# Two-layer decoder trunk on one core: all of GpSimd's transfers move to SyncE's queue, the convolution's columns are requested first, and the pool of big tiles has 24 places, not 22

## The chip, the core and the metric

The kernel runs on one core of a Trainium2 chip. The core has a matrix engine (TensorE, PE in the profile; its weight loads are PEld), a vector engine (VectorE, DVE), a scalar engine (ScalarE, ACT), GpSimd (POOL) and SyncE (SP), which here only issues transfers. Each engine takes its instructions in the order of the program; a name with a q (SPq, ACTq) is the engine's queue, where transfers are issued and waits are kept. All transfers run on the same 16 DMA engines. The metric is the time of one execution on the device in microseconds (us); compared are medians of several runs.

## What is computed

Two layers over 256 tokens of width 1024. Layer 0 mixes tokens with a convolution module, layer 1 with causal attention; beside it each has attention into 256 memory tokens. Each is followed by a projection, a norm, a mixture of experts (4 groups of 8, the best group and in it the best two experts per token) and a second norm.

```python
for i in range(DEPTH):                       # DEPTH = 2
    if i % 2 == 0:
        u = x @ conv_w_in                    # gated, then 31 taps along the tokens, norm, silu
        y_mix = conformer_conv(u[..., :2 * MIX_WIDTH], conv_dw_w, conv_dw_b, conv_ln_g, conv_ln_b)
    else:
        u = x @ moba_w_in
        y_mix = moba_attention(q, k, v)      # causal; one block of 256 tokens
    y_mem = memory_attention(q_mem, mem_k, mem_v)
    y = concatenate([y_mix, y_mem]) @ w_o[i]
    x = layer_norm(ALPHA * x + y, ln1_g[i], ln1_b[i])
    f = hierarchical_moe(x, w_rg[i], b_rg[i], w_re[i], b_re[i], w_gate[i], w_up[i], w_down[i])
    x = layer_norm(ALPHA * x + f, ln2_g[i], ln2_b[i])
```

All 64 experts are computed on slots of tokens, so every weight is read: 3 x 2 MB for an expert, 447 MB in all.

## The kernel before

**The pool and the loads.** Weights come in loads of 1 MB, each into a tile of 128 x 2048 numbers from one pool, `big`, of NB = 22 tiles (L41, L91). Activations take tiles from the same pool (`act`, L150). The order of loads is a list (`want`, L249 to L274): six tiles of the convolution's input weights, the memory tokens, four tiles around them, four of w_o (14 loads up to here), the gains, then the experts of layer 0, and so on for layer 1. A load is issued at the earliest point of the program at which a tile is sure to be free at every later point: the program is walked once without issuing anything, which leaves for each point the number of loads that may be out, NB less the tiles that activations hold plus the tiles that are done with (L147, L80), lowered to the least of all later points; `pump` (L137) then issues up to that number. By this count 14 loads may be out from the start until the third gated block of the convolution, and 37 of the first layer's when the norm ahead of its experts is done. Loads 16 to 39 are those of four experts whose number is fixed (kind "s"); load 40 is the first whose expert is chosen at run time, so that it waits for the numbers `eid`, which VectorE writes at L1208, and is let into the list by `opened` (L1209).

**Queues.** The weights, the input `raw`, the tokens `xn` and the router's weights are issued by SP. ScalarE issues one transfer: the convolution's columns (L552: taps, bias, gains, 204 KB), after the first two casts of the input and ahead of the first cast of a weight (`split`, L344), which TensorE's first matmuls (L405) need. GpSimd issues the rest: in the convolution stage the gated activations `h` of each of three blocks go to a buffer `hd` in DRAM (L597, two transfers a block) and come back shifted as `hs` (L617, eight a block), for the matmuls at L626 (`conv`). The program calls conv(0) and conv(1) in the middle of block 2, conv(2) and conv(3) after the memory keys, conv(4) and conv(5) between the two attentions into memory. GpSimd also writes the memory keys and values to DRAM (L722), from where layer 1 loads them.

**The tokens.** `xn` is loaded at L685, behind the router's weights (`router_load`, L324), and first used by `residual` (L498, with matmuls at L496).

**The branch.** In the middle of each layer's experts (after group 4) stands a branch (L1395) on the count of experts with more tokens than slots. Its body (`overflow`, L1251) holds up to seven more experts, whose weights GpSimd loads in 512-wide pieces (L1290).

Of the kernel before, what the change touches and what calls it, by code (L numbers as in the profile page):

```python
# [9 lines left out]
BF = mybir.dt.bfloat16  # L10
# [3 lines left out]
OP = mybir.AluOpType  # L14
# [3 lines left out]
S = 256  # L18
D = 1024
NT = S // 128  # L20
# [3 lines left out]
P = 128  # L24
MIX = 768
MC = MIX // 128
# [11 lines left out]
NEG = -1e30  # L38
FAR = 1e5
HW = 288  # L40
NB = 22  # L41
LATE = 1
NQ = 7
REST = (5, 6, 8, 10)
# [41 lines left out]
def body(ctx, tc, ahead, xT0, xs, memT, w_mem_kv, conv_w_in, conv_cols, moba_w_in, w_o, gains, w_r,  # L86
# [159 lines left out]
    raw = act("raw")  # L246
    for h in range(2):
        nc.sync.dma_start(raw[:, h * 1024:(h + 1) * 1024], xT0[:, h * 1024:(h + 1) * 1024])
    for b in range(3):  # L249
        for i in range(2):  # L250
            want(("cv", b, i), load(conv_w_in, 2 * b + i))
# [36 lines left out]
    nc.vector.tensor_scalar(alpha, ident, ALPHA, None, op0=OP.mult)  # L288
    upper = t1("upper")
    nc.vector.tensor_scalar(upper[:, :P], diff[:, :P], 0.0, None, op0=OP.is_gt)  # L290
    cmask = keep.tile([P, P], BF, name="cmask")
    nc.vector.tensor_scalar(cmask, upper[:, :P], NEG, None, op0=OP.mult)
    ident_b = keep.tile([P, P], BF, name="ident_b")
    nc.vector.tensor_copy(ident_b, ident)
    upper_b = keep.tile([P, P], BF, name="upper_b")
    nc.vector.tensor_copy(upper_b, upper[:, :P])
    ones_b = keep.tile([P, P], BF, name="ones_b")
# [120 lines left out]
    def attend(items, causal, room=None):  # L418


        n0 = 128 if causal else 256
        spans = [(0, n0), (n0, n0 + 256)]
        heads = []
        for qT, kT, v, put in items:
            two = [pb(), pb()]
            for s_ in two:
                if causal:
                    for a, b in spans:
                        nc.tensor.matmul(s_[:, b - P:b], lhsT=ident_b, rhs=cmask, start=a == 0, stop=False)
            for t in range(NT):  # L430
                a, b = spans[t]
                cuts = [(a, b - P), (b - P, b)] if causal else [(a, b)]
                for c, d in cuts:
                    for hh, s_ in enumerate(two):
                        r = slice(hh * HD, (hh + 1) * HD)
                        if d > c:
                            nc.tensor.matmul(s_[:, c:d], lhsT=qT[r, t * P:(t + 1) * P], rhs=kT[r, c - a:d - a],
                                             start=not causal and t == 0, stop=t == NT - 1 and d == b)
            heads += two
        done_ = []  # L440
        pr_ = room() if room else act("apr").rearrange("p (h s) -> p h s", h=4)
        for s_ in heads:
            st = small([P, 8], "ast", bufs=4)
            pr = pr_[:, len(done_)]
            for t in range(NT):
                a, b = spans[t]
                nc.vector.tensor_reduce(st[:, t:t + 1], s_[:, a:b], axis=AX.X, op=OP.max)
            nc.vector.tensor_scalar(st[:, 2:4], st[:, 0:2], -1.0, None, op0=OP.mult)
            for t in range(NT):
                a, b = spans[t]  # L450
                nc.scalar.activation(pr[:, a:b], s_[:, a:b], AF.Exp, bias=st[:, 2 + t:3 + t],
                                     scale=1.0, accum_out=st[:, 4 + t:5 + t])
            done_.append((st, pr))
        for st, pr in done_:
            nc.vector.reciprocal(st[:, 6:8], st[:, 4:6])
            for t in range(NT):
                a, b = spans[t]
                nc.vector.tensor_scalar(pr[:, a:b], pr[:, a:b], st[:, 6 + t:7 + t], None, op0=OP.mult)
        blocks = [(kt, t) for kt in range(2) for t in range(NT) if not causal or kt <= t]
        for i in range(len(items)):  # L460
            yield
            for hh in range(2):
                pr = done_[2 * i + hh][1]
                p_ = pb()
                for n, (kt, t) in enumerate(blocks):
                    a = spans[t][0] + kt * P
                    nc.tensor.transpose(p_[:, n * P:(n + 1) * P], pr[:, a:a + P], ident)
                n = len(blocks)
                evac(pr[:, :n * P], p_[:, :n * P])
        yield  # L470
        for i, (qT, kT, v, put) in enumerate(items):
            y_ = pb()
            for t in range(NT):
                kts = [kt for kt, t_ in blocks if t_ == t]
                for kt in kts:
                    n = blocks.index((kt, t))
                    for hh in range(2):
                        r = slice(hh * HD, (hh + 1) * HD)
                        nc.tensor.matmul(y_[r, t * P:(t + 1) * P], lhsT=v[:, kt, r],
                                         rhs=done_[2 * i + hh][1][:, n * P:(n + 1) * P], start=kt == kts[0],  # L480
                                         stop=kt == kts[-1])
            put(y_[:, :256])
        if not room:
            free()
# [56 lines left out]
    def conv_layer():  # L541
        acc = Acc()
        xT = parted(raw, "xT", (nc.scalar.copy, nc.vector.tensor_copy))
        free()
        cv_ = act("cv")
        cv = cv_[:, :MC * S].rearrange("p (c s) -> p c s", c=MC)
        npc, nwr = MC * (CW + 5), MC * 32
        cols = cv_[:, MC * S:MC * S + npc + nwr]
        pct = cols[:, :npc].rearrange("p (c k) -> p c k", c=MC)
        wrc = cols[:, npc:].rearrange("p (c b q) -> p c b q", c=MC, b=4)  # L550
        id32 = cv_[:, 2048 - 32:]
        nc.scalar.dma_start(cols, conv_cols)  # L552
        hd = dr.tile([MC, P * HW], F32, name="hd")
        wdg, hsrc, hs = {}, {}, {}

# [18 lines left out]
        def glu(b):  # L574
# [19 lines left out]
                nc.vector.tensor_mul(h[:, CW - 1:CW - 1 + S], p_[:, k], sg[:, k])  # L594
                hsrc[2 * b + i] = h
            for i in range(2):
                nc.gpsimd.dma_start(hd[2 * b + i].rearrange("(p s) -> p s", p=P), hsrc[2 * b + i])  # L597
            shifted(b)

        def last_taps(b):  # L600
# [11 lines left out]
        def shifted(n):  # L612

            for c in (2 * n, 2 * n + 1):
                hs[c] = act("hs")[:, :4 * HW].rearrange("p (b s) -> p b s", b=4)
                for r in range(4):
                    nc.gpsimd.dma_start(hs[c][32 * r:32 * r + 32, :, :HW - 4],  # L617
                                        view(hd[c, r:], [[HW, 32], [32 * HW, 4], [1, HW - 4]]))

        def conv(c):  # L620
# [17 lines left out]
        mT = parted(held("mem"), "mT")  # L638
        done("mem")
        taps(1)  # L640
        glu(2)

        p_ = pb()
# [36 lines left out]
        next(ats[0])  # L680
        conv(4)
        router_load(0)
        for t in range(NT):
            for half in range(2):
                nc.sync.dma_start(xn[t][half], xs[t, half])  # L685
        feed.ahead(2)
        next(ats[1])
        conv(5)
# [30 lines left out]
                                           op1=OP.mult, accum_out=col[:, t:t + 1])  # L719
        rsqrt(col[:, 2:4], col[:, 0:2])  # L720
        for i, v in enumerate((memk, memv)):
            nc.gpsimd.dma_start(kvd[:, i * 512:(i + 1) * 512].rearrange("p (c s) -> p c s", c=2), v)  # L722
        for a in ats:
            next(a)
        for a in ats:
# [317 lines left out]
    def moe(l, mixer, after=None):  # L1043
# [207 lines left out]
        def overflow():  # L1251
# [26 lines left out]
            def one_more(q):  # L1278
# [2 lines left out]
                sq = so[:, 4:8] if q else so[:, 0:4]  # L1281
                gather(one_hot(sq), xg=xo)
                pt = spots_turned(spots(sq))
                r = nc.gpsimd.value_load(ids[0:1, q:q + 1], min_val=l * NE, max_val=l * NE + NE - 1)

                def piece(src):
                    count[0] += 1
                    i = count[0] % 3
                    t_ = t2("wpc") if i == 2 else room[:, J * P + i * 512:J * P + (i + 1) * 512]
                    nc.gpsimd.dma_start(t_, src)  # L1290
                    return t_

                def up_piece(a):
# [183 lines left out]
```

## Time and profile before

| | |
|---|---|
| median of 3 runs | 1175.22 us (1174.49 to 1183.54) |
| the profiled execution | 1182.57 us, of which its span 1180.9 us |
| granted TensorE clock, mean | 0.947 |
| busy: PE, PEld, DVE, ACT, POOL | 1028.2, 722.3, 366.4, 210.5, 60.6 us |
| bytes moved | 447.16 MB, mean 379 GB/s over the span |

The page shows the span in 40 slices of 29.5 us. Busy PE is no proof of a bound by PE, since a matmul that waits for its weights inside the pipeline counts as busy; which limit holds in a stage is read from the bytes per slice and from the waits. The convolution stage lasts to about 160 us, the first experts to about 590, the attention stage to about 735, the second experts to the end.

### The profile page before, as it was taken

Reading aid. Unit: us, or ns where it says so; the run is one execution under the profiler, and the core shown is the slowest. Engines: PE = TensorE matmul, PEld = TensorE weight load, DVE = VectorE, ACT = ScalarE, POOL = GpSimd, SP = SyncE. Lnnn points to the kernel's source line nnn. Section 1 sums busy time; section 2 is a strip of 40 time slices with the busy share of each in tenths; the row PEclk is TensorE's granted clock in tenths of the full one; section 3 lists DMA queues with packets and bytes.
Section 4 is the critical chain, followed back from the end, with each engine's and each line's share of the span. In section 5 each row is a group of like instructions: output and inputs, shape, how many; then the busy total and the mean of one; then the engine's idle time right before and its main releaser. Section 6 shows DMA issues by size and latency. Waiting matters only on the chain. (4 is left out here: it accounts for less than half of the span.)

```text
span 1180.9 us, 26574 instructions
## 1 busy us (share of the span) xinstructions
PE 1028.2 (87%) x11292; PEld 722.3 (61%) x11292; DVE 366.4 (31%) x936; ACT 210.5 (18%) x456; POOL 60.6 (5%) x152
## 2 busy tenths in 40 slices
PE   1998999999889998866589998999997999996775
PEld 1986766665565575544469986666545656654542
DVE  3576832221121121111065765222211211221103
ACT  2314411111010010001044532011010111110000
POOL 1440200000000000000020002000000000000001
PEclk9999989999999999889899997999998999997777
DMA  9686969999999999999997386999999999999994
GB/s 381 235 282 265 347 251 419 424 424 426 425 424 425 427 424 425 426 426 425 425 427 271 108 293 252 384 425 424 426 427 422 425 427 425 424 426 425 426 425 177
DMA packets 63656, 447.16 MB, mean 379 GB/s; under 512 B 7656, under 2 KB 8040, under 8 KB 10280
## 3 DMA queue, kind: packets, MB, share of 16 engines
q1 hardware_dynamic: 61640, 439.73, 90.2%
q0 software_dynamic: 1600, 4.90, 1.5%
q8 instruction: 92, 1.51, 0.5%
q10 hardware_dynamic: 288, 0.73, 0.2%
q14 instruction: 36, 0.29, 0.1%
HBM read 442.87 MB, written 2.46 MB: 377 GB/s over the span
## 5 line engine op out<-in xcount | busy, mean ns | idle before, releaser
L974 PE MATMUL pb<-w,xg 128*32 128x128 f32 (+2 forms) x6528 | 400.1, 323 | 87.3 <-DMA w<-in_w_gate_dram 51.0
L974 PEld LDWEIGHTS pb<-w,xg 128*32 128x32 f32 (+2 forms) x6528 | 276.6, 123 | 208.9 <-issue 82.8
L1026 PE MATMUL pb<-w,hT 128*32 128x256 f32 (+1 forms) x1600 | 157.5, 432 | 7.8 <-DMA w<-in_w_down_dram 3.1
L1026 PEld LDWEIGHTS pb<-w,hT 128*32 128x32 f32 (+1 forms) x1600 | 74.5, 116 | 62.9 <-issue 36.5
L1031 ACT COPY o<-pb 32x256 f32<-32x256 f32 (+2 forms) x104 | 43.2, 416 | 367.1 <-DVE o L1031 232.5
L405 PE MATMUL pb<-xT,hl 128*128 128x256 f32 x672 | 86.0, 290 | 25.8 <-ACT hl L344 25.6
L1031 DVE COPY o<-pb 32x256 f32<-32x256 f32 (+2 forms) x104 | 49.8, 478 | 177.6 <-PE pb L1026 157.7
L998 DVE TENSOR_TENSOR h<-pb,h 128x128 f32<-128x128 f32 (+2 forms) x64 | 22.9, 358 | 253.8 <-PE pb L974 246.8
L405 PEld LDWEIGHTS pb<-xT,hl 128*128 128x128 f32 x672 | 84.0, 198 | 27.3 <-ACT hl L344 25.6
L496 PE MATMUL pa<-o,pt 128*128 128x512 f32 x192 | 92.7, 628 | 3.5 <-DVE o L1031 2.0
L950 PEld LDWEIGHTS pb<-oh,xn 128*128 128x128 f32 x704 | 80.6, 192 | 7.4 <-issue 7.4
L950 PE MATMUL pb<-oh,xn 128*128 128x128 f32 x704 | 84.0, 278 | 0.0
L345 DVE TENSOR_TENSOR hl<-w,hl 128x1024 fp32r<-128x1024 f32 x53 | 63.1, 1221 | 36.0 <-ACT hl L344 33.1
L496 PEld LDWEIGHTS pa<-o,pt 128*128 128x128 f32 x192 | 37.7, 207 | 44.5 <-issue 32.4
L344 ACT CAST hl<-w 128x1024 fp32r<-128x1024 f32 x54 | 54.7, 1053 | 33.3 <-DMA w<-in_memT_dram 19.3
L992 ACT ACTIVATE h<-pb 128x128 f32<-128x128 f32 (+2 forms) x64 | 21.2, 331 | 195.9 <-PE pb L974 195.0
L128 POOL TENSOR_SCALAR lmv<-lmv 128x1 f32<-128x1 f32 x8 | 1.7, 216 | 1027.7 <-DVE lmv L506 1026.0
L496 PE MATMUL pa<-hl,y 128*128 128x512 f32 x192 | 46.0, 395 | 0.0
L125 DVE COPY hT<-pb 128x128 f32<-128x128 f32 (+2 forms) x32 | 11.4, 358 | 105.1 <-PE pb L1004 81.2
L123 ACT COPY xg<-pb 128x512 f32<-128x512 f32 x22 | 12.9, 586 | 160.4 <-PE pb L950 160.4
L496 PEld LDWEIGHTS pa<-hl,y 128*128 128x128 f32 x192 | 35.5, 188 | 8.0 <-issue 0.5
L1238 DVE TENSOR_SCALAR ow<-iota,sm,sw 128x128 f32<-128x128 f32 x96 | 26.8, 343 | 19.2 <-PEq L1395 13.3
(229 smaller groups left out, 705.9 us busy)
## 6 DMA issues: line engine op xcount, KB each, us to landing
w<-in_w_gate_dram SPq DMA_DIRECT2D x128, 1024.0 KB, 19.5
w<-in_w_up_dram SPq DMA_DIRECT2D x128, 1024.0 KB, 19.5
w<-in_w_down_dram SPq DMA_DIRECT2D x128, 1024.0 KB, 19.5
w<-in_moba_w_in_dram SPq DMA_DIRECT2D x10, 1024.0 KB, 18.4
w<-in_w_o_dram SPq DMA_DIRECT2D x8, 1024.0 KB, 19.8
w<-in_conv_w_in_dram SPq DMA_DIRECT2D x7, 1024.0 KB, 15.4
w<-in_gains_dram SPq DMA_DIRECT2D x4, 1024.0 KB, 12.4
hs<-hd POOLq DMA_DIRECT2D x24, 142.0 KB, 3.2
```

What stands on the lines that cost most here:

```text
L123: nc.scalar.copy(o, i)
L344: nc.scalar.copy(hi, src)
L345: eng.tensor_sub(lo, src, hi.bitcast(F32))
L405: nc.tensor.matmul(o, lhsT=lhs(a, j), rhs=rhs(b, j), start=k == 0, stop=k == 3 * n - 1)
L496: nc.tensor.matmul(self.at[t][half], lhsT=lhsT, rhs=rhs, start=start, stop=stop)
L950: nc.tensor.matmul(p_[:, j - jj], lhsT=now(t, j), rhs=oh[t], start=t == 0, stop=t == NT - 1)
L974: nc.tensor.matmul(o_[b * n:(b + 1) * n, :], lhsT=self.xs[:, j, :], rhs=wj[:, pairs(b) if fw == P else slice(b * fw, (b + 1) * fw)], start ...
L992: nc.scalar.activation(self.h[:, :fw], g_, AF.Silu)
L998: nc.vector.tensor_mul(self.h[:, :fw], u_, self.h[:, :fw])
L1026: nc.tensor.matmul(ds[0][b * n:(b + 1) * n, :dw], lhsT=chunk(c), rhs=wd(c, b * dw, (b + 1) * dw), start=c == 0, stop=c == 3)
L1031: (nc.scalar.copy if 2 * b >= m else nc.vector.tensor_copy)(o[lo:lo + n, b * D // m:(b + 1) * D // m], ds[b] if nb == 1 else ds[0][b * n:( ...
L1238: nc.vector.tensor_scalar(o_[:, t], iota, sm[:, i:i + 1], sw[:, 4 + i:5 + i], op0=OP.is_equal, op1=OP.mult)
```

## The change

The columns' tile is taken and its transfer issued ahead of the list of loads, still by ScalarE. The transfers of `h`, `hs` and the memory keys and values, and the pieces and the expert's number in the overflow's body, are issued by SP. The tokens are requested in the program after the taps of block 1, ahead of the third gated block, and no longer behind the router's weights. NB is 24. The scratch space that transfers issued by GpSimd need in every partition is set to 256 bytes, which makes room for the two tiles. The causal mask is added as a product of -1e30 times the identity and a 0/1 triangle, not of the identity and a triangle of -1e30; one tile of constants is gone.

```diff
-NB = 22
+NB = 24
...
     raw = act("raw")
     for h in range(2):
         nc.sync.dma_start(raw[:, h * 1024:(h + 1) * 1024], xT0[:, h * 1024:(h + 1) * 1024])
+    cv_ = act("cv")
+    ncol = MC * (CW + 5), MC * 32
+    nc.scalar.dma_start(cv_[:, MC * S:MC * S + sum(ncol)], conv_cols)
     for b in range(3):
...
-    cmask = keep.tile([P, P], BF, name="cmask")
-    nc.vector.tensor_scalar(cmask, upper[:, :P], NEG, None, op0=OP.mult)
-    ident_b = keep.tile([P, P], BF, name="ident_b")
-    nc.vector.tensor_copy(ident_b, ident)
+    neg_b = keep.tile([P, P], BF, name="neg_b")
+    nc.vector.tensor_scalar(neg_b, ident, NEG, None, op0=OP.mult)
...
-                        nc.tensor.matmul(s_[:, b - P:b], lhsT=ident_b, rhs=cmask, start=a == 0, stop=False)
+                        nc.tensor.matmul(s_[:, b - P:b], lhsT=neg_b, rhs=upper_b, start=a == 0, stop=False)
...
-        cv_ = act("cv")
...
-        nc.scalar.dma_start(cols, conv_cols)
...
-                nc.gpsimd.dma_start(hd[2 * b + i].rearrange("(p s) -> p s", p=P), hsrc[2 * b + i])
+                nc.sync.dma_start(hd[2 * b + i].rearrange("(p s) -> p s", p=P), hsrc[2 * b + i])
...
-                    nc.gpsimd.dma_start(hs[c][32 * r:32 * r + 32, :, :HW - 4],
+                    nc.sync.dma_start(hs[c][32 * r:32 * r + 32, :, :HW - 4],
...
         taps(1)
+        for t in range(NT):
+            for half in range(2):
+                nc.sync.dma_start(xn[t][half], xs[t, half])
         glu(2)
...
         router_load(0)
-        for t in range(NT):
-            for half in range(2):
-                nc.sync.dma_start(xn[t][half], xs[t, half])
...
-            nc.gpsimd.dma_start(kvd[:, i * 512:(i + 1) * 512].rearrange("p (c s) -> p c s", c=2), v)
+            nc.sync.dma_start(kvd[:, i * 512:(i + 1) * 512].rearrange("p (c s) -> p c s", c=2), v)
...
-                r = nc.gpsimd.value_load(ids[0:1, q:q + 1], min_val=l * NE, max_val=l * NE + NE - 1)
+                r = nc.sync.value_load(ids[0:1, q:q + 1], min_val=l * NE, max_val=l * NE + NE - 1)
...
-                    nc.gpsimd.dma_start(t_, src)
+                    nc.sync.dma_start(t_, src)
...
-    nc = _bacc.Bacc("TRN2", target_bir_lowering=False, num_devices=1)
+    nc = _bacc.Bacc("TRN2", target_bir_lowering=False, num_devices=1, dynamic_dma_scratch_size=256)
```

## Rows read from the trace of the kernel before

**Rows 1.** The page, GB/s moved in each of 40 slices of the span

```profile
GB/s 381 235 282 265 347 251 419 424 424 426 425 424 425 427 424 425 426 426 425 425 427 271 108 293 252 384 425 424 426 427 422 425 427 425 424 426 425 426 425 177
```

**Rows 2.** The chain that ended last, two pieces: start us, us, what

```profile
979.18 19.04 DMA w<-in_w_down_dram
...
1143.53 19.41 DMA w<-in_w_down_dram
```

**Rows 3.** Timeline of SP, its first waiting issues: start us, us, line, out<-in, count

```profile
9.40 0.33 SPq L183 DMA_DIRECT2D w<-in_conv_w_in_dram  x1
...
14.26 7.74 SPq L183 DMA_DIRECT2D w<-in_w_o_dram  x4
```

**Rows 4.** Queues (packets, MB, share); issues (KB, median us to landing); hs min/median/max

```profile
q0 software_dynamic: 1600, 4.90, 1.5%
...
w<-in_w_gate_dram SPq DMA_DIRECT2D x128, 1024.0 KB, 19.5
...
hd<-h POOLq DMA_DIRECT2D x6, 144.0 KB, 2.1
...
DMA to landing us min/median/max: 2.7/3.2/8.0
```

**Rows 5.** Timeline of the start, ACT and PE, with idle time and its releaser

```profile
24.09 0.38 ACTq L552 DMA_DIRECT2D cv<-in_conv_cols_dram  x1
24.50 5.78 ACT L344 CAST hl<-w 128x1024 fp32r<-128x1024 f32 x6 [19.27 <-DMA w<-in_memT_dram]
...
25.60 31.77 PE L405 MATMUL pb<-xT,hl 128*128 128x256 f32 x240 [25.60 <-ACT hl L344]
```

**Rows 6.** Timeline of the convolution's blocks, POOL, PE and SP

```profile
41.80 1.33 POOL L597 DMA_DIRECT2D hd<-h  x2 [37.95 <-DVE h L594]
...
44.72 4.49 POOL L617 DMA_DIRECT2D hs<-hd  x8 [1.57 <-ACT hl L344]
...
57.30 6.25 PE L626 MATMUL pb<-hs,wdg 128*32 128x256 f32 x112
...
60.59 0.33 SPq L189 DMA_DIRECT2D w<-in_gains_dram  x1
...
75.18 6.25 PE L626 MATMUL pb<-hs,wdg 128*32 128x256 f32 x112
```

**Rows 7.** The wait for xn, and busy us, clock, DMA share, GB/s behind it

```profile
99.82 5.40 PE L496 MATMUL pa<-xn,alpha 128*128 128x512 f32 x8 [3.25 <-DMA xn<-in_xs_dram]
...
100.00:102.00 2.00, 2.00 (x3) 0.78 (x4) 2.00 (x3) 0.77 (x1) 0.00 (x0) 0.52 1.03 367
```

**Rows 8.** Timeline at the first layer's gate: SP's issues, and the expert numbers

```profile
138.94 9.21 SPq L213 DMA_DIRECT2D w<-in_w_up_dram  x2
...
160.00 3.02 SPq L213 DMA_DIRECT2D w<-in_w_down_dram  x2
...
160.81 0.18 DVE L1208 TENSOR_SCALAR eid<-pb 1x32 int32<-1x32 f32 x1 [4.86 <-PE pb L1201]
...
166.52 2.07 SPq L213 DMA_DIRECT2D w<-in_w_gate_dram  x2
```

**Rows 9.** Busy us by engine, clock, DMA share and GB/s ahead of that gate

```profile
156.00:160.00 4.00, 4.00 (x28) 2.90 (x27) 0.00 (x0) 1.17 (x2) 0.00 (x0) 0.74 0.00 0
```

**Rows 10.** Timeline of SP at the second layer's gate

```profile
710.88 10.20 SPq L213 DMA_DIRECT2D w<-in_w_up_dram  x2
733.10 3.02 SPq L213 DMA_DIRECT2D w<-in_w_down_dram  x2
```

**Rows 11.** The branch at L1395: duration ns min/median/max, first and last start; SP's issues

```profile
L1395 POOLq INC_SWDGE_SEM  x2: 801/812/822, 166.2 to 739.2; - x2
L1395 SPq COMPARE_BRANCH  x2: 45/49/53, 309.3 to 882.1; - x2
...
L1395 PEldq COMPARE_BRANCH  x2: 6038/6090/6142, 311.2 to 884.7; - x2
...
308.92 8.95 SPq L213 DMA_DIRECT2D w<-in_w_up_dram  x2
```

More of the change, by code (lines that the diff above doesn't have):

```diff
@@ L544, in conv_layer @@
         free()
-        cv_ = act("cv")
         cv = cv_[:, :MC * S].rearrange("p (c s) -> p c s", c=MC)
[L547 to L550, printed above, removed]
+        cols = cv_[:, MC * S:MC * S + sum(ncol)]
+        pct = cols[:, :ncol[0]].rearrange("p (c k) -> p c k", c=MC)
+        wrc = cols[:, ncol[0]:].rearrange("p (c b q) -> p c b q", c=MC, b=4)
         id32 = cv_[:, 2048 - 32:]
-        nc.scalar.dma_start(cols, conv_cols)
         hd = dr.tile([MC, P * HW], F32, name="hd")
```

## The prediction

> **What bounds the kernel now.** I read four views, from the whole to the stage. First the page's bytes per slice of 29.5 us [rows 1]: counted from 0, 419 to 427 GB/s in slices 6 to 20 and again in 26 to 38, lower in 0 to 5 and 21 to 25. So the transfers bound both expert stages, and something else bounds the convolution stage (0 to about 160 us) and the attention stage (about 590 to 740). The chain that ended last says the same of the end: from 979 us it is one load after the other [rows 2], with a tail of 18 us of compute behind the last landing at 1162.94. In an expert stage the end is the moment the transfers became continuous plus the bytes still to come. A microsecond counts where it moves that moment, or where it makes the transfers idle inside the stage.
>
> Second, the start. SP issues its first transfers at once, later ones only as earlier ones land: from 9.40 to the last of the four for w_o, at 14.26 + 7.74 - 0.33 = 21.67, are five steps of 2.45 us [rows 3]. A load in this queue lands 19.5 us after its issue in the median [rows 4], eight times 2.45. So eight are in flight, in order. ScalarE is caught by the same limit: its request for the convolution's columns stands at 24.09 us, after 19.27 us in which ScalarE waited for the memory tile's landing, although the weights it casts next had long arrived. TensorE's first matmul is at 25.60 [rows 5].
>
> Third, the convolution stage itself: TensorE works almost without a pause from 25.6 us, with one wait of 3.25 us for the tokens xn [rows 7]. Fourth, the gate of the expert stage: SP's load 38 waits for the first expert's matmuls until 160.00 [rows 8], and from 156 to 160 nothing moves at all [rows 9]. All 39 loads that need no routing would fill it, but 22 tiles let only 37 go. The second layer repeats the pattern: issues end at 721.08, the next is at 733.10 [rows 10].
>
> **The change, part by part.** Columns first. Requested before anything is in flight, they wait for nothing; their 204 KB delay the first weight by 0.5 us at 425 GB/s. SP's issue at 9.40 is the one that waits for that weight, so it lands at 9.4 now and at 9.9 then. From the first cast to the first matmul are 1.10 us (24.50 to 25.60) [rows 5]. TensorE starts at 11.0: 14.6 us earlier. Weights arrive every 2.45 us and the first convolution matmul comes 31.7 us after the start for five tiles, so TensorE stays the limit.
>
> Transfers from GpSimd to SP. Before, h goes to DRAM at 41.80 on GpSimd's own queue and lands in 2.1 us [rows 4, 6], the eight shifted copies follow at 44.72, and the first convolution needs them at 57.30: over 5 us to spare. Then, h is ready at 41.80 - 14.6 = 27.2, but SP's program has 16 loads ahead of it (14 before, two more by the pool). The ninth issues when the first has landed, at 9.9, the 16th seven steps on, at 27.1, and h's two parts in the next two places, 29.5 and 32.0. In the queue they stand behind all 16 loads: the 16th lands at 9.9 + 15 x 2.45 = 46.7, h at 46.7 + 0.7 = 47.4 (2 x 144 KB). Only then may SP issue the eight copies, at 0.4 us each (0.33 for the instruction in [rows 3], and the step between two), and the first four have landed 2.1 to 3.2 us after the fourth is out [rows 4]: 51.3. TensorE stands at the first convolution at 57.30 - 14.6 = 42.7. It waits 8.6 us, and the start's gain is 6.0 from there on. Bounds: 0 if h overtakes the loads, 14 if the copies take the 8.0 us that one of them took at most. I take the sum, as every row of that queue shows order. The Trainium skill, DMA: Bandwidth & Descriptors, section "Issuing engines are not separate DMA queues", says that which engine issues matters only for the time of the issuing sequencer. By that rule this move is free and the sum 8.6 us better; it is the second rival.
>
> The later copies are late too, but covered: blocks 1 and 2 are ready on SP by about 60 and 75 us, and their convolutions come at 75.18 - 6 = 69 [rows 6] and later. Loads queued behind them on SP wait with them; load 17 goes at about 59, while load 15, which had its place, went at 60.59 [rows 6], so no weight is later than before. The memory keys and values (kvd) stand behind a copy that is done before the loads behind it may go. GpSimd loses 32 issues of about 0.55 us, on an engine that nobody waits for here.
>
> Tokens earlier. Their four issues move from behind the router's weights to behind block 1's copies, about 58 us, and land 30 us before use: the 3.25 us go [rows 7]. The granted clock was 0.52 in the 2 us after that wait, close to the lower of its two levels (1.2 of 2.4 GHz): 1 us lost. The new wait of 8.6 us may cost the same; I let the two cancel.
>
> Two more tiles. At each point of the program two more loads are out. Loads 38 and 39 go where 36 and 37 went (138.94 and about 148), and fill 4.9 us of the idle stretch [rows 8, 9]. Load 40 needs the expert numbers, written at 160.81 to 160.99, and goes at about 161.8, 1.8 us after load 38 went. But the issues behind it are paced by TensorE (166.52), so in the old order the transfers paused twice more; laid out load by load at 2.45 us, 43 loads are through at 172.9 then against 41 at 172.7 now. Gain 4.7 us (bounds 4.9 - 1.8 = 3.1 and 4.9). The second gate is the same: 4.7 again.
>
> SP in the branch. The overflow's pieces now hang on SP, inside the branch at L1395. GpSimd, which had them, settles a transfer counter after the skipped body (0.8 us), SP has only a compare of 49 ns, and TensorE, whose body is long, stands 6.1 us [rows 11]. SP now has a long body and counters to settle while eight loads are in flight. If that settling must wait until they have landed, the queue runs empty once per layer. An empty queue costs 0.4 us of issue and the overhead of a small transfer, 2.1 - 0.35 = 1.75, with some settling: 3 us. Below: 0, as SP stands there anyway, 8.95 us around the issue of 308.92, under 19.5 us of loads in flight. Above: 6.1 us of standing behind the drain as well, 9 us. No row shows it. I take 3, because the counters of landed and skipped transfers are the same ones, and the standing would pass while the loads land. Twice: 6.
>
> The mask's product uses other operands with the same shapes and count, and one vector instruction less, at 2 us, where VectorE waits for the input until 5.4: nothing. The overflow's pieces themselves don't run where no expert overflows; the trace has no transfer of them, and the routing is the same.
>
> Sum: - 14.6 + 8.6 - 3.25 - 2 x 4.7 + 2 x 3 = - 12.65 us. The profiled execution took 1182.57 us (span 1180.9, 1.7 around it), 7 us above the median of the three runs; 1.07% of the median 1175.22 is 12.6: 1162.6 us.
>
> **The rivals.** (a) The branch is free: 6 us better, 1156.6. For it: SP's stop there is covered now. Against: it had no transfers in the body. (b) The move of the copies is free: 8.6 better, 1154 with the branch at 3, 1148 without. For it: the queue that goes carried only 4.90 MB of 447 [rows 4]. Against: the 19.5 us of every load in SP's queue. (c) The branch costs 9 each, standing behind the drain: 12 worse, 1174.6, no change. For it: TensorE's 6.1 us. (d) On the other side: the branch costs more than 9.3 us per layer, (14.6 - 8.6 + 3.25 + 9.4) / 2, from where the change loses. Drain and restart (3), standing (6.1) and a settling of 0.8 for each of the eight transfers in flight (6.4), one after the other, are 15.5: twice that less 18.65 is + 12.4, 1187.5. Against: the parts would have to follow one another, none under the 19.5 us of loads in flight.
>
> **How the numbers follow.** The forecast (8.6 us of waiting, branch at 3) 0.38, with its own range of 1157 to 1168; (a) 0.25; (b) 0.08; (c) 0.13; (d) 0.08, from its turning point on; something not listed 0.08. One per cent, about what a measurement of this kernel can tell from no change, is 1163.5 and 1187.0. Of the forecast 0.21 lies below the first and 0.17 above, since its parts are uncertain by a few us; (a) and (b) lie below, (c) within, (d) half within and half above the second; of what is not listed 0.02 within and 0.06 above. Faster 0.54, within 0.36, slower 0.10. The range leaves out the lower half of (b), most of (d) and what is not listed, under 0.2: 1150 to 1177.
>
> **What would show it.** In the changed kernel's trace: the first matmul at about 11 us, not 25.6 (if not, the wait on ScalarE was another). A wait of TensorE for the copies at L626, near 43 us and 8.6 long; none means (b). The residual's matmuls at L496 without a wait for xn. A stop of the transfers ahead of each gate [rows 9] that is some 3 us shorter (it begins 4.9 later and ends 1.8 later). A dip in the GB/s in the middle of each expert stage (about 300 and 870 us): none is (a), 3 us is the forecast, 9 is (c). The prediction fails if the convolution stage is held by something behind SP's order that I priced at nothing, above all the router's loads or block 2's copies, or if the expert stages don't start with the transfers two loads ahead.

## The result, and the profile after

The changed kernel takes 1168.33 us (median, 1165.21 to 1174.27) where the kernel before, measured beside it, takes 1179.72: a ratio of 0.9898, 95% interval 0.988 to 0.9917, or 12.0 us of 1180. The prediction was 0.9893 (12.65 us). Its profiled span is 1167.4 us, 13.5 under that of before. Below, a ratio is always to the kernel before measured beside the kernel in question, and one thousandth is 1.18 us.

The start. Timeline of ScalarE's queue and of TensorE, with the idle time ahead and its releaser, against [rows 5] and [rows 6]:

```profile
0.74 0.40 ACTq L251 DMA_DIRECT2D cv<-in_conv_cols_dram  x1
10.27 30.56 PE L406 MATMUL pb<-xT,hl 128*128 128x256 f32 x240 [10.27 <-ACT hl L345]
52.55 8.97 PE L624 MATMUL pb<-hs,wdg 128*32 128x256 f32 x112 [11.73 <-DMA hs<-hd]
...
94.48 3.70 PE L497 MATMUL pa<-xn,alpha 128*128 128x512 f32 x8
```

TensorE starts 15.3 us earlier, then stands 11.73 us for block 0's copies; the tokens need no wait. SP's timeline in that stretch:

```profile
27.32 0.33 SPq L213 DMA_DIRECT2D w<-in_w_gate_dram  x1
29.82 2.75 SPq L595 DMA_DIRECT2D hd<-h  x2
47.90 3.64 SPq L615 DMA_DIRECT2D hs<-hd  x8
```

and one line of its waits up to 60 us (total, times, longest us):

```profile
SPq L615 <- DMA hd<-h: 18.4, 2, 15.2
```

h is requested at 29.82 and has landed only at 47.90: SP's next instruction, the first shifted copy, waits 15.2 us for it behind sixteen loads. Before, on GpSimd's queue, the same step took from 41.80 to 44.72 [rows 6]. Behind TensorE's wait the clock is low (window, busy us of PE, PEld, DVE, ACT, POOL, granted clock, DMA share, GB/s):

```profile
50.00:60.00 10.00, 7.45 (x88) 4.16 (x92) 0.42 (x1) 0.00 (x0) 0.00 (x0) 0.59 0.78 195
```

0.59 is nearer the lower of the two levels (1.2 of 2.4 GHz), and the 112 matmuls of the convolution take 8.97 us, not 6.25.

The first gate, against [rows 8] and [rows 9]: timeline of VectorE and SP.

```profile
151.99 0.18 DVE L1206 TENSOR_SCALAR eid<-pb 1x32 int32<-1x32 f32 x1 [3.08 <-PE pb L1199]
153.25 0.96 SPq L213 DMA_DIRECT2D w<-in_w_gate_dram  x2
```

Two windows around it, columns as above:

```profile
148.00:152.00 4.00, 4.00 (x38) 2.92 (x38) 0.81 (x8) 1.17 (x2) 0.00 (x0) 1.00 0.00 0
152.00:156.00 4.00, 2.12 (x20) 1.16 (x22) 3.44 (x18) 1.87 (x3) 0.00 (x0) 1.00 0.44 102
```

The expert numbers are there 8.8 us earlier, and the next load goes 1.26 us after them.

The branch, in the middle of each expert stage. First the page's GB/s by slice, against [rows 1]:

```profile
GB/s 388 305 309 289 369 280 426 424 426 426 364 392 425 426 425 426 425 426 425 425 427 348 110 294 268 412 426 425 426 427 346 424 426 426 424 425 426 426 424 215
```

The view of the branch's line (duration ns, first and last start), against [rows 11]:

```profile
L1393 SPq EVENT_SEMAPHORE  x18: 17/17/17, 304.7 to 890.1; - x18
```

SP's waits from 280 to 345 us:

```profile
SPq L1393 <- SPq L1393: 20.1, 4, 10.2
```

The timeline of ScalarE and SP behind the first stop:

```profile
320.19 0.28 ACT L990 ACTIVATE h<-pb 128x128 f32<-128x128 f32 x1 [18.01 <-SPq L1393]
...
320.56 0.34 SPq L213 DMA_DIRECT2D w<-in_w_down_dram  x1
```

And windows of 1 us around it:

```profile
316.00:317.00 1.00, 0.00 (x0) 0.00 (x0) 0.00 (x0) 0.00 (x0) 0.00 (x0) 0.50 0.58 246
317.00:318.00 1.00, 0.00 (x0) 0.00 (x0) 0.00 (x0) 0.00 (x0) 0.00 (x0) 0.50 0.37 156
318.00:319.00 1.00, 0.00 (x0) 0.00 (x0) 0.00 (x0) 0.00 (x0) 0.00 (x0) 0.50 0.10 41
319.00:320.00 1.00, 0.00 (x0) 0.00 (x0) 0.00 (x0) 0.00 (x0) 0.00 (x0) 0.50 0.02 8
320.00:321.00 1.00, 0.48 (x12) 0.44 (x16) 0.00 (x0) 0.28 (x1) 0.00 (x0) 0.50 0.00 0
321.00:322.00 1.00, 1.00 (x24) 0.91 (x20) 0.00 (x0) 0.00 (x0) 0.00 (x0) 0.50 0.49 90
322.00:323.00 1.00, 1.00 (x28) 0.89 (x20) 0.00 (x0) 0.00 (x0) 0.00 (x0) 0.50 0.82 238
323.00:324.00 1.00, 1.00 (x28) 0.89 (x24) 0.00 (x0) 0.00 (x0) 0.00 (x0) 0.50 1.02 426
```

Slices 10 and 30 now have a hole. SP stands 20.1 us settling nine counters (18 in two layers): the instructions in the view, by which it is taken to make up for the transfers that the skipped body did not issue. Meanwhile its queue runs empty. The busy shares of the eight windows from 316 to 324 sum to 3.40 us, so 4.6 us of transfer are lost here; and ScalarE waits 18.01 us for SP's last counter, TensorE with it. In the second layer the shares of 0.79, 0.24 and 0.94 in three windows of 4 us from 884 give 4.1 us.

### The profile page after: what moved, and what is told of

The parts are those of the page before. It is cut to its first block, busy times and chain, and to the rows that moved or that the text cites. A ratio compares the mean times of both kernels' runs of the same rounds, so it can differ in the third digit from the quotient of the medians.

```text
span 1167.4 us, 26547 instructions
## 1 busy us (share of the span) xinstructions
PE 1026.1 (88%) x11292; PEld 720.4 (62%) x11292; DVE 364.4 (31%) x935; ACT 210.7 (18%) x456; POOL 42.3 (4%) x120
## 3 DMA queue, kind: packets, MB, share of 16 engines
HBM read 442.87 MB, written 2.46 MB: 381 GB/s over the span
## 5 line engine op out<-in xcount | busy, mean ns | idle before, releaser
L972 PEld LDWEIGHTS pb<-w,xg 128*32 128x32 f32 (+2 forms) x6528 | 279.6, 125 | 205.2 <-issue 80.9
L1024 PE MATMUL pb<-w,hT 128*32 128x256 f32 (+1 forms) x1600 | 160.8, 444 | 5.1 <-ACT hT L123 2.1
L497 PE MATMUL pa<-o,pt 128*128 128x512 f32 x192 | 88.4, 604 | 3.5 <-DVE o L1029 2.0
L345 ACT CAST hl<-w 128x1024 fp32r<-128x1024 f32 x54 | 54.9, 1053 | 18.4 <-PE pb L406 10.1
## 6 DMA issues: line engine op xcount, KB each, us to landing
w<-in_w_gate_dram SPq DMA_DIRECT2D x128, 1024.0 KB, 19.5
w<-in_w_up_dram SPq DMA_DIRECT2D x128, 1024.0 KB, 19.5
w<-in_w_down_dram SPq DMA_DIRECT2D x128, 1024.0 KB, 19.5
w<-in_moba_w_in_dram SPq DMA_DIRECT2D x10, 1024.0 KB, 19.6
w<-in_gains_dram SPq DMA_DIRECT2D x4, 1024.0 KB, 19.5
```

The lines of the kernel that those rows point to most:

```text
L345: nc.scalar.copy(hi, src)
L497: nc.tensor.matmul(self.at[t][half], lhsT=lhsT, rhs=rhs, start=start, stop=stop)
L972: nc.tensor.matmul(o_[b * n:(b + 1) * n, :], lhsT=self.xs[:, j, :], rhs=wj[:, pairs(b) if fw == P else slice(b * fw, (b + 1) * fw)], start ...
L1024: nc.tensor.matmul(ds[0][b * n:(b + 1) * n, :dw], lhsT=chunk(c), rhs=wd(c, b * dw, (b + 1) * dw), start=c == 0, stop=c == 3)
```

## The experiments: the columns and the copies

**The columns alone.** The kernel before with one edit:

```diff
+    cv_ = act("cv")
+    ncol = MC * (CW + 5) + MC * 32
+    nc.scalar.dma_start(cv_[:, MC * S:MC * S + ncol], conv_cols)
     for b in range(3):
...
-        nc.scalar.dma_start(cols, conv_cols)
```

> The kernel before, with one part of the change alone: the columns' tile is taken and its transfer issued ahead of the loads; everything else (GpSimd's transfers, 22 tiles, tokens late) as before. Theory (the copies were late in the changed kernel because they stand in SP's queue behind 16 loads): here they go through GpSimd's queue, so TensorE starts at about 10.3 us, does not wait at L626 for more than about 2 us, still waits for the tokens some 3 us, and the time is about 15 us under before, 0.987. Rival (the copies are late because the transfers themselves are slow while the loads run, whatever the queue): a wait of 8 to 12 us at L626 here too, and only 3 to 5 us gained, 0.997.

Measured: 0.9942 (0.992 to 0.9964), between the two. Timeline of TensorE and GpSimd:

```profile
10.57 31.76 PE L408 MATMUL pb<-xT,hl 128*128 128x256 f32 x240 [10.57 <-ACT hl L347]
46.45 7.94 PE L627 MATMUL pb<-hs,wdg 128*32 128x256 f32 x112 [4.13 <-DMA hs<-hd]
92.35 5.13 PE L499 MATMUL pa<-xn,alpha 128*128 128x512 f32 x8 [4.93 <-DMA xn<-in_xs_dram]
33.35 4.38 POOL L618 DMA_DIRECT2D hs<-hd  x8 [5.26 <-DMA hd<-h]
```

The copies' issues (KB each, median us to landing):

```profile
hs<-hd POOLq DMA_DIRECT2D x24, 142.0 KB, 7.8
hd<-h POOLq DMA_DIRECT2D x6, 144.0 KB, 6.2
```

15.0 us are won at the first matmul. Then the copies come late on GpSimd's queue too: they now run while the loads are still in flight and land in 6.2 and 7.8 us, where they took 2.1 and 3.2 before [rows 4]. TensorE waits 4.13 us for them, loses 1.7 to the clock (7.94 for 6.25), and waits 4.93 for the tokens. The residual starts at 92.35, 7.5 us ahead of before: half of the 15 us is lost again in the convolution stage with the copies on GpSimd's queue. In the changed kernel it is 10.0 of the 15.3 (94.48 against 99.82).

**The columns late, all else changed.** The changed kernel, with the columns requested where they were before:

```diff
-    nc.scalar.dma_start(cv_[:, MC * S:MC * S + sum(ncol)], conv_cols)
...
         id32 = cv_[:, 2048 - 32:]
+        nc.scalar.dma_start(cols, conv_cols)
```

> The changed kernel with one part undone: the columns are requested where the kernel before requested them. Theory (the columns' 14.6 us and the copies' wait belong together: with the late start h comes at 41.8, the copies land at about 51, before they are needed at 57): first matmul at 25.6, no wait for copies, no wait for the tokens, so against the kernel before only the tokens (-4), the tiles (-6.5) and the branch (+5.5) are left: ratio 0.995 to 0.996, 6 to 7 us slower than the changed kernel. Rival (the columns are worth their full 14.6 us): ratio 1.002.

Measured: 0.9936 (0.9911 to 0.9961): 4.5 us slower than the changed kernel, near the 6 to 7 of the theory and not 15. One number was not foreseen. Timeline of SP, ScalarE and TensorE:

```profile
8.80 0.33 SPq L183 DMA_DIRECT2D w<-in_conv_w_in_dram  x1
...
25.97 0.33 SPq L213 DMA_DIRECT2D w<-in_w_gate_dram  x1
28.44 0.38 ACTq L550 DMA_DIRECT2D cv<-in_conv_cols_dram  x1
28.86 5.79 ACT L344 CAST hl<-w 128x1024 fp32r<-128x1024 f32 x6 [23.86 <-DMA w<-in_conv_w_in_dram]
29.95 30.41 PE L405 MATMUL pb<-xT,hl 128*128 128x256 f32 x240 [29.95 <-ACT hl L344]
60.29 6.25 PE L624 MATMUL pb<-hs,wdg 128*32 128x256 f32 x112
```

The first matmul is at 29.95, not 25.6. ScalarE's request goes out 2.47 us after SP's sixteenth load, as it went 2.42 us after the fourteenth before (21.67 in the prediction, 24.09 in [rows 5]). The trace names one landing as what released it: here that of the load issued at 8.80, which lands after 19.6 us; before, that of the memory tile [rows 5], issued at 4.87 and landed after 19.2. In both kernels this is the transfer eight places ahead of the request in the order of the program, counted over SP's queue and ScalarE's together. The two loads of the two new tiles stand ahead of the request too, and so it waits for a later landing: 4.35 us more. And the convolution needs no wait at 60.29: h is requested only at 44.26, when most loads have landed, and SP's first copy goes at 47.49. Start and copies are one account: whoever starts early waits for the copies.

**Ten loads ahead of block 0's copies.** The changed kernel, with the loads behind the tenth held until block 0's copies are issued:

```diff
-        while todo and ahead and use["loads"] < ahead[max(len(trace) - 1, 0)]:
+        while todo and ahead and use["loads"] < min(use["hold"], ahead[max(len(trace) - 1, 0)]):
...
                     nc.sync.dma_start(hs[c][32 * r:32 * r + 32, :, :HW - 4], ...)
+            use["hold"] = 1 << 30
+            pump()
```

> The changed kernel, with only 10 of the 16 first loads issued ahead of block 0's h and its copies; the other six follow them. Nothing else differs. Theory (queue order): h lands about 32 us, the copies by 37, TensorE does not wait at L626 and its clock does not fall behind the wait: 11.7 + 2.7 = 14.4 us under the changed kernel, 1154, ratio to before 0.978. Rival (SP's own work, issue by issue, or slow copies make them late): the wait stays above 6 us and less than 6 us are gained.

Measured: 0.9858 (0.9831 to 0.9886), 4.7 us better than the changed kernel and less than expected. Timeline of TensorE:

```profile
41.22 6.25 PE L626 MATMUL pb<-hs,wdg 128*32 128x256 f32 x112
63.31 7.58 PE L626 MATMUL pb<-hs,wdg 128*32 128x256 f32 x112 [4.13 <-DMA hs<-hd]
82.26 5.32 PE L626 MATMUL pb<-hs,wdg 128*32 128x256 f32 x56 [3.62 <-DMA hs<-hd]
```

Block 0's wait of 11.73 us is gone, at the full clock: loads ahead in the same queue were its cause. But the loads that were held are now let go between block 0 and block 1, and blocks 1 and 2 wait 4.13 and 3.62 us behind them, with 3.4 us of low clock (7.58 for 6.25, 5.32 for 3.23). My expectation had looked at block 0 alone.

**The tokens, with the copies on GpSimd.** The kernel with the columns alone, and the four requests for xn moved:

```diff
         taps(1)
+        for t in range(NT):
+            for half in range(2):
+                nc.sync.dma_start(xn[t][half], xs[t, half])
         glu(2)
```

> The kernel before with the columns first and the tokens requested behind block 1's copies; the copies stay on GpSimd's queue, 22 tiles, no transfer of SP in the branch. Theory (in the kernel with the columns alone, 4.9 us of the gain went to the wait for the tokens and 1.4 to the clock behind it): no wait for xn, ratio 0.989 against 0.994 with the columns alone. Rival (the wait for the tokens is only the first of two, and the next load is as late): 0.994.

Measured: 0.9856 (0.9824 to 0.9888), against 0.9942 with the columns alone: 10.1 us, of which the two intervals leave 4 to 16. The 4.93 us of the wait and the 1.4 us of clock behind it make 6.3, and in the traces the residual starts 6.6 us earlier (85.79 against 92.35); what the medians show beyond that is not accounted for. Timeline of TensorE:

```profile
85.79 3.70 PE L499 MATMUL pa<-xn,alpha 128*128 128x512 f32 x8
```

The residual runs without a wait at the full clock; the wait for block 0's copies stays (3.36 us). With SP's branch as it was, 22 tiles and the copies on their own queue, this kernel is no slower than the changed one (0.9898).

## The experiments: the tiles

```diff
-NB = 24
+NB = 22
```

> The changed kernel with 22 tiles, not 24. Theory: 14 loads and not 16 stand ahead of h, so the wait at L626 is two loads shorter, 11.7 - 4.9 = 6.8 us, and the stage gains about 5; each gate loses two loads, 4.7, as forecast: 5 less 9.4 makes it 4 to 5 us slower than the changed kernel, 1172 to 1173, ratio to before about 0.994. Rival (the tiles bring nothing at the gates, since the two layers' expert stages in the changed kernel came out only 0.1 and 0.5 us shorter): it is 5 us faster than the changed kernel, 0.985.

Measured: 0.9953 (0.9933 to 0.9974), as expected. The two tiles bring 6.5 us net, and the net has two sides. With two loads fewer ahead of the copies TensorE waits 6.92 us, not 11.73:

```profile
47.93 8.07 PE L624 MATMUL pb<-hs,wdg 128*32 128x256 f32 x112 [6.92 <-DMA hs<-hd]
```

That is 4.8 us, two times 2.4, that the two tiles cost in the convolution stage. What they give in the expert stages shows in this table, from the first write of the expert numbers (eid) to the first load of the attention stage, and in layer 1 to the last scatter (the product of o and pt at the end), in us, over all fourteen profiled kernels:

| tiles; transfers on SP in the branch | layer 0 | layer 1 |
|---|---|---|
| 22; none (before, columns alone, tokens) | 412.3, 412.8, 412.5 | 431.2, 433.6, 432.7 |
| 22; all | 416.7 | 434.5 |
| 24; eight or all (changed, columns late, ten ahead, eight, staged) | 410.1 to 412.3 | 430.2 to 431.1 |
| 24; none, one or four (the five others) | 406.4 to 407.8 | 426.0 to 427.2 |

Without the branch's price two more tiles shorten a stage by 4.5 to 6.4 us in layer 0 and 3.9 to 7.6 in layer 1. The spread within a line, up to 2.4 us, is that of single profiles.

## The experiments: the branch

**No transfer in the branch.**

```diff
-                r = nc.sync.value_load(ids[0:1, q:q + 1], ...)
+                r = 0
...
-                    nc.sync.dma_start(t_, src)
+                    nc.gpsimd.memset(t_, 0.0)
```

> The changed kernel, with no transfer in the branch's body: the overflow's pieces are filled by GpSimd with zeros (the part left out: the weights of overflow experts, a body that no token enters here). Theory (SP settles the counters of eight transfers in flight and so lets the queue run empty once per layer): no dip in the GB/s around 300 and 870 us, SP does not stand at the branch, 4.6 + 4.1 = 8.7 us under the changed kernel, 1159.6, ratio to before 0.982. Rival (the dip is made up later, because TensorE stands at the branch for 6 us itself and the loads behind it have no tile to go to): under 2 us gained.

Measured: 0.9853 (0.9826 to 0.988), 5.3 us under the changed kernel. The page's GB/s have no hole in slices 10 and 30:

```profile
GB/s 388 309 308 293 371 276 426 425 424 426 425 423 428 425 425 425 425 427 424 425 426 316 110 302 256 416 426 425 425 427 422 425 426 425 425 425 425 425 425 189
```

That shows where the hole comes from, not which property of the transfers makes it: their settling or the length of the body. The next three leave only the first one, four or eight transfers on SP:

```diff
-                    nc.sync.dma_start(t_, src)
+                    if count[0] <= 1:             # 1, 4, 8
+                        nc.sync.dma_start(t_, src)
+                    else:
+                        nc.gpsimd.memset(t_, 0.0)
```

**One.**

> The changed kernel with only the first transfer of the overflow's pieces left on SP in the branch; the others are filled with zeros on GpSimd (left out of the computation, on a path that these inputs don't reach). Theory (one transfer in the body is enough to make SP wait until its queue is empty): SP stands 18 to 20 us at the branch as in the changed kernel, the GB/s dip by 4 to 5 us in slices 10 and 30, ratio 0.990 to the kernel before. Rival (the price is the long body, so it goes with the number of transfers skipped): a stop under 5 us, no dip, ratio 0.985.

Measured: 0.9819 (0.9794 to 0.9844). The theory as I had put it fell: one transfer doesn't empty the queue. SP waits 7.3 us for TensorE behind the branch, as without transfers (7.6), and 1.5 us at the branch itself, and slice 10 moves 424 GB/s. SP's wait at the branch from 280 to 345 us:

```profile
SPq L1396 <- SPq L1396: 1.5, 2, 1.4
```

**Four.**

> The same with four transfers left on SP. Theory: five counters to settle, so SP waits for the fourth load of the eight in flight, about 10 us, of which 6 to 8 lie beside the wait for TensorE's branch that is there anyway; four loads remain in flight, so the transfers never stop: no dip, ratio 0.982 to 0.986. Rival (any wait at the branch empties the queue, or the price goes with each transfer): a dip of half the size, 0.986 to 0.988.

**Eight.**

> The changed kernel with the first eight transfers of the overflow's pieces left on SP in the branch; the others are filled with zeros on GpSimd (left out of the computation, on a path that these inputs don't reach). Theory (each skipped transfer has to be settled on one of the counters that the loads in flight use, and a counter is settled only when its load has landed; with one transfer SP settled two counters, with all of them nine): eight transfers touch them all, so SP stands 18 to 20 us as in the changed kernel, the GB/s dip in slices 10 and 30, ratio 0.988 to 0.990. Rival (the price goes with the length of the body): hardly a stop beyond TensorE's, no dip, 0.982 to 0.985.

Measured: 0.9825 (0.9802 to 0.9849) with four, 0.9898 (0.9876 to 0.9919) with eight, the changed kernel's own ratio. One and four stand 9.3 and 8.6 us under it, none at all (0.9853) only 5.3, with an interval that reaches from 2 to 9; the three intervals overlap, so that no difference among them is shown. The counters that SP settled (over two layers) in the view of the branch's line, first with one transfer:

```profile
L1396 SPq EVENT_SEMAPHORE  x4: 17/17/17, 298.9 to 872.1; - x4
```

with four:

```profile
L1396 SPq EVENT_SEMAPHORE  x10: 17/17/17, 299.2 to 875.1; - x10
```

and with eight:

```profile
L1396 SPq EVENT_SEMAPHORE  x18: 17/17/17, 301.7 to 895.8; - x18
```

SP's wait there from 280 to 345 us, with four:

```profile
SPq L1396 <- SPq L1396: 9.9, 5, 3.1
```

and with eight:

```profile
SPq L1396 <- SPq L1396: 19.9, 4, 14.5
```

and two windows of the hole with eight:

```profile
316.00:320.00 4.00, 0.00 (x0) 0.00 (x0) 0.00 (x0) 0.00 (x0) 0.00 (x0) 0.50 0.63 264
320.00:324.00 4.00, 2.37 (x47) 2.12 (x50) 0.00 (x0) 0.28 (x1) 0.00 (x0) 0.50 0.31 74
```

Two, five, nine and nine counters for one, four, eight and all transfers: one per transfer up to eight, and one more. The wait is 1.5 us with one, 9.9 with four, four landings of 2.45, and 19.9 with eight, the 19.5 us that a load takes in this queue [rows 4]. That is what one expects if a counter is settled only when the load that last used it has landed; no view shows a counter and its load side by side, so the mechanism is argued from the counts and the times. With four transfers the transfers never stop; with eight the queue is empty. No part of the body's length shows: eight transfers cost as much as all of them (0.9898 both).

## The experiments: versions that go further

**Loads held in steps, no pieces.** The edit of the ten loads, with a step for each block, on top of the kernel without pieces:

```diff
+            use["hold"] = (12, 14, 1 << 30)[n]
+            pump()
```

> The changed kernel without transfers in the overflow's body (its pieces are filled with zeros on GpSimd; that part of the computation, which these inputs don't reach, is left out) and with the loads held in steps: 10 before block 0's copies, 12 before block 1's, 14 before block 2's, all others behind those. Theory (what costs time are loads that stand ahead of a copy in SP's queue, in every block): with at most two loads, 4.9 us, ahead of a copy, TensorE has no wait for copies at any of the three convolution groups, the residual starts about 71 us after the first matmul, near 81 us instead of 93.75, and the time is about 12 us under that of the kernel without pieces: 0.975 of the kernel before. Rival (the stop only moves, to the weights that are held back): the residual or the router's stage waits for loads and the time stays at 0.985.

Measured: 0.9727 (0.9702 to 0.9752), 14.9 us under the kernel without pieces. TensorE waits at none of the three blocks, and the residual starts at 80.93:

```profile
80.93 3.70 PE L497 MATMUL pa<-xn,alpha 128*128 128x512 f32 x8
```

**The same steps on the changed kernel, branch and all.**

> The changed kernel with one thing added: the loads held in steps of 10, 12 and 14 ahead of the copies of blocks 0, 1 and 2. Theory (copies and branch are two separate costs): the convolution stage as short as in the staged kernel without pieces, the dips in slices 10 and 30 as in the changed kernel, ratio 0.978 to 0.981, about 12 us under the changed kernel. Rival (the two share a cost, so that the stage's gain is lost in the branch): 0.985 or more.

Measured: 0.9806 (0.9781 to 0.9832), 10.9 us under the changed kernel; the residual starts at 80.82, and slices 10 and 30 have their holes (347 and 336 GB/s). Copies and branch are two separate costs.

**The same steps, the pieces back on GpSimd.** The whole computation:

```diff
-                r = nc.sync.value_load(ids[0:1, q:q + 1], ...)
+                r = nc.gpsimd.value_load(ids[0:1, q:q + 1], ...)
...
-                    nc.sync.dma_start(t_, src)
+                    nc.gpsimd.dma_start(t_, src)
```

> The whole computation: the changed kernel with the loads held in steps of 10, 12 and 14 ahead of the copies of blocks 0, 1 and 2, and with the overflow's pieces (and the register they need) back on GpSimd's queue; 24 tiles. Theory (the price in the branch belongs to SP's queue alone): no dip, the convolution stage without a wait for copies, ratio 0.973 as without pieces. Rival (a transfer in the body stops the loads whoever issues it): dips in slices 10 and 30 and 0.978 to 0.982.

Measured: 1149.82 us, 0.9741 (0.9716 to 0.9767), the best of the whole kernels, 18.5 us under the changed one.

```profile
GB/s 388 248 326 416 344 416 426 423 428 426 424 424 426 426 425 426 425 426 424 426 416 236 137 328 216 424 424 425 426 427 422 426 426 425 424 426 425 426 425 184
```

No hole: the price in the branch is that of SP's queue, on which the loads are. GpSimd reaches the branch at 138.9 us and settles its counters from 141.6 on, with nothing of its own in flight and long before SP gets there (286.1); which of the two spares it is not told apart.

## Why the prediction came out, step by step

**The start** was predicted at -14.6 us and is -15.3, with the first matmul at 10.27 (11.0 predicted). The cause that I gave, the landing of the memory tile, fits: that tile lands at 24.07 (4.87 and 19.2), and the request goes at 24.09. In the kernel with late columns the same count of eight places names a later load, issued at 8.80 and landed at 28.4, and the request goes at 28.44; my expectation there had not counted the two new loads.

**The copies' wait** was predicted at 8.6 us and is 11.73. Its construction holds in each place: the sixteenth load issued at 27.32 (27.1 predicted), h at 29.82 (29.5), the copies after 47.90 (47.4), the convolution at 52.55 (51.3). Of the 3.1 us that the term is larger, 1.9 come from TensorE, which was there at 40.82, not 42.7 (it started 0.7 us earlier and ran its 240 matmuls in 30.56 us, not 31.77), and 1.25 from copies that were that much later. The rival that the move is free, with no wait at all, is out. The Trainium skill, DMA: Bandwidth & Descriptors, section "Issuing engines are not separate DMA queues", says that the issuing engine makes no difference beyond its own issuing time. For a single transfer the traces don't agree: with 14 loads ahead of both, SP's first copy waits 15.3 us for h to land (22 tiles), GpSimd's 5.26 (columns alone). For the stage they nearly agree: on GpSimd's queue h lands in 6.2 us beside the loads, not 2.1, the copies in 7.8, not 3.2, and the convolution starts at 46.45, on SP's queue at 47.93. What I had missed is this comparison at equal loads. Of the 11.73 us 4.13 are waited on GpSimd's queue too, once TensorE starts early; 2.8 more come with SP's queue (6.92), though only 1.5 by the time at which the convolution starts; and 4.8 come with the two loads more. The prediction had put all of its 8.6 us down to the move. With 16 loads ahead no run has the copies on GpSimd's queue.

**The clock** was left out on the ground that two losses of about 1 us cancel. The new loss is 2.7 us at the convolution, and the one that went is 1.7, not 1. It was paid back elsewhere: the residual of the tokens takes 3.70 us, not 5.40 [rows 7], and a gather of 16 matmuls ahead of the gate 2.02 us, where TensorE's timeline of before has

```profile
154.27 3.75 PE L929 MATMUL pb<-oh,xn 128*128 128x128 f32 x16 [0.48 <-DVE prs L1174]
```

At the expert numbers the sum of all this is -8.8 us, where the prediction has -14.6 + 8.6 - 3.25 = -9.25.

**The tokens** need no wait, as predicted.

**The tiles** were predicted at 4.7 us per stage. The table gives 4.9 and 5.2 us for the kernel without pieces against before: right in size. The sign that went with it did not come: the stop of the transfers ahead of a gate is not 3 us shorter. By the DMA shares of windows of 1 us, 8.6 us of transfer are lost before (from 152 to 162) and 8.7 in the changed kernel (145 to 155); at the second gate 9.0 (725 to 735) and 8.3 (715 to 725). Against the expert numbers the first stop ends 1.6 us later, about as forecast (1.8), but begins only 1.5 later, not 4.9: load for load, the loads ahead of it came 12.3 us earlier (7.4, and two loads more), the numbers only 8.8. What makes up the rest of the 4.9 and 5.2 us is not shown.

**The branch** is the term that was mis-sized: 3 us per layer predicted, 4.8 and 4.7 found by the table (the changed kernel's 412.2 and 430.7 against 407.4 and 426.0 without pieces; from 2.3 to 5.9 over all pairs of the table's last two rows), 4.6 and 4.1 by the windows. That the settling waits for the loads in flight, and that SP's own standing passes meanwhile, fits what was found. What the 3 us lacked is the end: the last load has landed by about 319, and SP's next goes at 320.56, with ScalarE and TensorE released at 320.19 and 320.52.

**The sum.** Both stages of experts together were predicted at 2 x (-4.7 + 3) = -3.4 us and give -0.1 and -0.5. The missing 2.8 us are made up by the clock: from the first load of the attention stage to the second gate the changed kernel takes 158.3 us, before took 160.8, since sixteen gather matmuls there run in 2.02 us, not 3.75, and eight transposes in 1.06, not 1.90; and the last scatter takes 3.70 us, not 5.36. In the profiled pair, - 8.82 - 0.07 - 2.46 - 0.47 is - 11.82 us at the last scatter and - 13.5 at the end of the span. So the mechanisms were right in the main, and the total is right partly by chance: two terms came out dearer, the copies' wait by 3.1 us and the branch by 3.5 in both layers together, and the clock, which I had put at nothing, came out 4.8 us in the change's favour (2.72 lost; 1.70, 1.73, 2.46 and 1.66 gained). Only the first two, the loss and the residual, stand beside waits that the change makes or takes away. The others fall either way: over the fourteen profiles the gather at the first gate takes the short time in eight (the kernel with eight transfers, the same there as the changed one, takes 3.75 us), at the second gate in six, and the last scatter takes 3.70 us in twelve. These 5.9 us belong to this pair of profiles; what they come to in the medians is not shown. The mask's product, priced at nothing, has no run of its own; both profiles have 11292 matmuls, and VectorE has 935 instructions where it had 936.

## What to carry to other kernels

A transfer that something waits for soon does not belong behind loads that nobody waits for yet: hold the loads back by number until the urgent ones are out, and do it for every later one too, or the stop moves one place on. Another queue alone did not do it here: beside 14 loads the copies on GpSimd's queue still cost 4.13 us of waiting. A branch that is hardly ever taken still has a price for the engine whose transfers stand in its body, as many in-flight transfers as the body has, up to the whole queue; such a body's transfers belong on an engine with nothing in flight. Starting earlier is worth only what the next thing needed can follow.

## What had not been expected of the hardware

Sixteen gather matmuls ahead of a gate take 2.02 or 3.75 us, in the same code, by the level of the clock. Timeline at the second gate, then a window around it, of the changed kernel:

```profile
717.81 2.02 PE L927 MATMUL pb<-oh,xn 128*128 128x128 f32 x16 [0.49 <-DVE prs L1172]
```

```profile
716.00:722.00 6.00, 5.51 (x48) 4.38 (x48) 2.09 (x15) 1.17 (x2) 0.00 (x0) 0.93 0.05 18
```

and the same two of the kernel with ten loads ahead, which does the same work there:

```profile
717.29 3.75 PE L929 MATMUL pb<-oh,xn 128*128 128x128 f32 x16 [0.48 <-DVE prs L1174]
```

```profile
716.00:722.00 6.00, 5.52 (x33) 4.81 (x34) 2.09 (x15) 1.17 (x2) 0.00 (x0) 0.55 0.03 11
```

The granted clock is 0.93 in the one and 0.55 in the other. From the first load of the attention stage to the second gate the fourteen profiles take 158.3 to 164.6 us, although none of the experiments edits that stage. What sets the level at such a place stays open. Single profiles stand some us off the medians in any case: the kernel without pieces is 8.9 us under the changed one by span and 5.3 by median, though in these two profiles the level is the same at both gates.

Not expected either: a request of ScalarE waits for the landing of a load eight places ahead in the program, though that load is in SP's queue (28.44 us for a request that was ready at about 5; whether the chip or the program sets the eight is not shown), and a body with eight transfers costs as much as one with all.
